# Attention heads in pairs, and gathered expert rows handed out during the one-hot stage

## The chip, the cores and the metric

The kernel runs on one core of a Trainium2 chip. The metric is the device time of one execution in microseconds; lower is better. The engines are named as in the profile: PE multiplies matrices (PEld is its loading of the stationary operand), DVE and ACT are the vector and the scalar engine, POOL is GpSimd, SP issues most transfers. Each engine works through its own instructions in a fixed order and waits on semaphores for the others. Rows of the profile give start and duration in us, or mean durations in ns where a column says so.

## What is computed

Two layers (l = 0, 1) of a hybrid trunk over 512 latent tokens of width 1024 with 256 context tokens. The context goes through layer 0 in full, and gives only keys and values to layer 1. Cut to what matters:

```python
ys, ysc = token_mixers(...)          # four kinds of attention, four heads of width 64 each:
#   y_na: neighbourhood, 512 + 256 keys, a bias per head      y_df: differential, two maps of width 32 a head
#   y_sw: sliding window of 128, with a sink                  y_gq: grouped heads, all 768 keys
x = x + g1 * merge_branches(h, ys, ...)
x = x + g2 * peer_ffn(h2, ...)       # a mixture of 16384 one-row experts
...
def peer_ffn(h, wq, keys, u, v):     # 8 heads, the best 16 experts of each token in each head
    a = gelu(einsum('td,thkd->thk', xb, u[eb]))
    return einsum('thk,thkd->td', gb * a, v[eb])
```

## The kernel before, in words

A tile is 128 tokens: the latents are tiles 0 to 3, the context is tiles 4 and 5. Everything is float32; products that need it are split into a high and a low part (`split`), so that one product is three matmuls: high by high, low by high, high by low.

**Order of the stages.** Context mixers, merge and output projection of layer 0; routing scores of the context; then for layer 0 and for layer 1 the latents' mixers, merge, output projection with norm, routing, a one-hot stage (`dense_weights`), and a dense stage (`dense`). A scheduler orders the instructions of each engine ahead of time by priorities and a simulated time line, not by the order of the program text. So a chain may be written one way and stand another way on the engine.

**Attention (`mixers`).** For each of the four kinds (`typ` 0 to 3, in the order of the reference above) there are two blocks of two heads. The two heads of a block lie in partitions 0 to 63 and 64 to 127 of the queries and keys. Before, the head (`sub`) is the outer loop and the query tile `i` the inner one. One step of a head is: `scores` (six matmuls of 64 contracted rows into the PSUM tile `sps`, three over the 512 latent keys and three over the 256 context keys), `softmax` (a maximum on DVE, an exponential on ACT into `prob`), a scaling of `prob` on ACT, and `pv` (six transposes of `prob` into the PSUM tile `mmps`, copies of these to `pT` by ACT and DVE, and six products of `pT` with the values, which write 64 partitions of the output bank). A float32 product stands as two PE instructions in the trace. There are two `sps` tiles, two `pT` and three `prob`. Kind 1 has two score maps per head, and combines them on DVE.

**Gathered work (`sparse`).** Tiles 4 and 5 (context) and tile 3 do the expert sum by gathering: 256 rows of 512 KB each per tile, 128 of u and 128 of v, fetched by an indirect transfer that POOL issues (line 828), and used by one DVE instruction each (line 839 for u, 841 and 843 for v). A piece is two rows. `tick(n, ins)` hands out n pieces at the place where it stands, and makes their gathers and their DVE instructions wait for the matmul `ins` (`pace`). Ticks stand after each head's `pv` (2.9 pieces, `TICK_A`), in the merge (2.7), and in the dense stage, which divides what is left evenly. The row buffers (`rows`, NROW = 8) hold gathered rows; row j + 8 can be fetched when row j is used. The same buffers hold the activations that layer 1's one-hot stage computes ahead (`acts_ahead`, two per buffer). At the start of layer 0's dense stage the rest of the context's rows and all of tile 3's are left. In layer 1 only tile 3's rows exist, and all of them fall in the dense stage.

**One-hot stage (`dense_weights`).** For tiles 0 to 2 it writes the matrix of expert weights to DRAM: 24 blocks of 16 tokens. Per block POOL makes eight one-hot rows (`oj`, line 895), DVE makes two wide `oj` (line 897) and twelve `oi` (line 907), ACT four `oi`, PE sixteen products (line 909). Beside it run the routing of the next tile on DVE and, in layer 0, the modulation of layer 1 (line 174, whose four quarters write partitions 0, 32, 64 and 96), in layer 1 the activations ahead.

**Dense stage (`dense`).** For each of 128 expert groups: 24 matmuls for the activation (lines 923 to 926, weights `ur`), 18 matmuls into the output (line 985, weights `vr`). `ur` and `vr` (512 KB each) are fetched by SP into three buffers, `wc` (1.5 MB) once in eight groups.

Of the kernel before, what the change touches and what calls it, by code (L numbers as in the profile page):

```python
# [23 lines left out]
GW = 64  # L24
# [9 lines left out]
TICK_M = 2.7  # L34
GS = 2
NROW = 8
# [3 lines left out]
def tile_hybrid_trunk(  # L40
# [235 lines left out]
    def na_bias(l, h, pool):  # L276
        t = pool.tile([P, 16, GW], FT, tag="bias", name="bias", bufs=1)
# [30 lines left out]
    def rope_apply(pool, src, tile_i, nh, dh, o, perm=False):  # L308
# [5 lines left out]
        t = pool.tile([P, 256], FT, tag="ropet", name="ropet")  # L314
# [6 lines left out]
        u = pool.tile([P, 256], FT, tag="ropeu", name="ropeu") if perm else o  # L321
# [28 lines left out]
    def head_scale(pool, src, r, nh, w, o, perm=False):  # L350

        u = pool.tile([P, 256], FT, tag="ropeu", name="ropeu") if perm else o
# [118 lines left out]
    def softmax(pool, S_, W, scale, bias=None, sinkc=None):  # L471

        pt = pool.tile([P, 768], FT, tag="prob", name="prob", bufs=3)
# [26 lines left out]
    def scores(q, r, i, keys, S_):  # L500
# [3 lines left out]
        for kh, kl, k0, n in keys:  # L504
            o = 0
            while o < n:
                step = min(512 - off % 512, n - o)
                k = slice(k0 + o, k0 + o + step)
                mm3(S_[:, off:off + step], q[0][r, t], q[1][r, t], kh[r, k], kl[r, k], True, True)
                off += step  # L510
                o += step
        return off

    def pv(pool, pt, W, vals, o, part, i, lean):

        nb = W // P
        pT = pool.tile([P, 6, P], FT, tag="pT", name="pT", bufs=2)
        b = 0
        while b < nb:
            n = min(4, nb - b)  # L520
            tp = mm_ps()
            for j in range(n):
                PE.transpose(tp[:, j * P:(j + 1) * P], pt[:, (b + j) * P:(b + j + 1) * P], ident)  # L523
            if b and nb > 2 and not lean:
                V.tensor_copy(pT[:, b:b + n, :], tp[:, :n * P].rearrange("p (a c) -> p a c", a=n))
            else:
                S.activation(pT[:, b:b + n, :], tp[:, :n * P].rearrange("p (a c) -> p a c", a=n), AF.Copy)
            b += n
        for j in range(nb):
            last = PE.matmul(o[part:part + 64, i * P:(i + 1) * P], vals[j], pT[:, j, :], start=(j == 0),  # L530
                             stop=(j == nb - 1))
        return last

    def mixers(l, pool, hh, hl, n_tiles, is_ctx, yd, fill):
# [3 lines left out]
        for typ in range(4):  # L538
# [4 lines left out]
            for blk in range(2):  # L543
# [4 lines left out]
                for sub in range(2):  # L548

                    h = blk * 2 + sub if typ < 2 else blk + 2 * sub  # L550
                    part = sub * 64
                    d = slice(part, part + 64)
                    cvals = [cvt[:, j, kb * P + part:kb * P + part + 64] for j in range(2)]
# [658 lines left out]
```

## Time and profile before

| | |
|---|---|
| median of 3 runs | 5221.3 us (5208.61 to 5224.62) |
| the profiled execution | 5226.89 us, its span 5225.1 us |
| busy in the span | PE 86%, DVE 73%, ACT 38%, POOL 34% |
| latents' mixers, layer 0 / layer 1 | 593 us / 440 us |
| one-hot stage, layer 0 / layer 1 | 247 us / 223 us |
| dense stage, layer 0 / layer 1 | 1163 us / 1003 us |

The stages follow each other with little overlap, so that each is read by itself: the busy time of an engine in the stage's window, against the window's length. A PE row's busy time includes the latency of a matmul's end, so the distance from one start to the next tells what a matmul costs in a stream. The granted clock of a window says how far PE ran at its higher level.

### The profile page before, as it was taken

How to read it: one execution, taken by the hardware profiler on the slowest of the kernel's cores; microseconds unless marked ns; L12 is line 12 of the kernel's file. 1: busy time of each engine (PE TensorE's matmuls, PEld its weight loads, DVE VectorE, ACT ScalarE, POOL GpSimd, SP SyncE). 2: the span in 40 equal slices, each digit the busy share in tenths (PEclk: the TensorE clock that was granted, in tenths of full speed). 3: DMA queues.
4: the chain of work that ended last, by engine and by line, in shares of the span. 5: the costliest groups of instructions: out<-in, count | busy, mean ns of one | idle time of the engine just before them, and what ended most of it. 6: DMA issues, size and time to landing. Idle time of an engine off the chain costs nothing.

```text
span 5225.1 us, 70074 instructions
## 1 busy us (share of the span) xinstructions
PE 4511.5 (86%) x24960; PEld 3935.3 (75%) x24960; DVE 3834.7 (73%) x8420; ACT 2008.0 (38%) x3323; POOL 1791.0 (34%) x1414
## 2 busy tenths in 40 slices
PE   6778885599675889999899979899986889999998
PEld 4577765477663678888788878788776779999997
DVE  3457878989979968887778855553479957777777
ACT  3344443242223643333233344452333743333333
POOL 0000045766613755455555400000002724444442
PEclk7788876799887999999999988799998999999999
DMA  5474256889943789998899831003332468888885
GB/s 192 131 189 158 65 204 225 306 291 349 366 149 133 255 296 333 326 353 310 306 316 343 308 115 40 19 25 104 126 115 77 166 208 316 300 301 309 299 306 208
DMA packets 558322, 1167.75 MB, mean 223 GB/s; under 512 B 79316, under 2 KB 329748, under 8 KB 551828
## 3 DMA queue, kind: packets, MB, share of 16 engines
q1 hardware_dynamic: 410516, 626.33, 36.5%
q0 software_dynamic: 147456, 536.94, 28.6%
q8 instruction: 197, 3.23, 0.2%
q14 instruction: 153, 1.25, 0.1%
HBM read 1090.97 MB, written 72.16 MB: 223 GB/s over the span
## 4 chain that ended last, share of the span: by engine, by line
PE 65%; DVE 15%; DMA 11%; issue 4%; ACT 3%; POOL 2%; SPq 0%; DVEq 0%; ACTq 0%; POOLq 0%
PE sps L985 12%; PE mmps L985 6%; PE mmps L152 6%; PE mmps L923 6%; PE mmps L153 6%; PE mmps L924 6%; PE mmps L154 6%; PE mmps L926 6%; DMA vr<-in_uv_dram 4%; PE mmps L530 3%; DVE rows L839 3%; PE sps L152 2%; POOL oj L895 2%; PE mmps L523 2%; DMA raw<-in_ada_w_dram 2%
## 5 line engine op out<-in xcount | busy, mean ns | idle before, releaser
L828 POOL DMA_INDIRECT rows<-in_uv_dram,idx x1024 | 1484.2, 1449 | 2057.9 <-PE mmps L530 694.9
L895 POOL TENSOR_SCALAR oj<-io,dwt 128x128 f32<-128x128 f32 x384 | 306.1, 813 | 1314.0 <-DVE bv L788 1027.5
L843 DVE SCALAR_TENSOR_TENSOR acc<-rows,gt,acc 128x1024 f32<-128x1024 f32 x508 | 650.6, 1281 | 143.3 <-PE mmps L926 140.3
L839 DVE SCALAR_TENSOR_TENSOR rows<-rows,h 128x1024 f32<-128x1024 f32 x512 | 605.0, 1221 | 146.0 <-PE mmps L926 121.9
L141 DVE TENSOR_TENSOR lo<-raw,hi 128x1024 fp32r<-128x1024 f32 x280 | 341.8, 1221 | 347.6 <-ACT hi L140 347.2
L140 ACT ACTIVATE hi<-raw 128x1024 fp32r<-128x1024 f32 x280 | 296.4, 1060 | 587.3 <-PE mmps L153 331.2
L140 ACT ACTIVATE vh<-vr 128x1024 fp32r<-128x1024 f32 x256 | 270.9, 1059 | 524.2 <-DMA vr<-in_uv_dram 235.2
L141 DVE TENSOR_TENSOR vl<-vr,vh 128x1024 fp32r<-128x1024 f32 x256 | 312.5, 1221 | 165.8 <-ACT vh L140 159.3
L140 ACT ACTIVATE uh<-ur 128x1024 fp32r<-128x1024 f32 x256 | 271.0, 1059 | 361.8 <-PE mmps L985 218.5
L923 PE MATMUL mmps<-p0h,uh 128*128 128x384 f32 x1024 | 351.1, 343 | 20.4 <-ACT uh L140 17.2
L141 DVE TENSOR_TENSOR ul<-ur,uh 128x1024 fp32r<-128x1024 f32 x256 | 312.8, 1222 | 60.6 <-ACT uh L140 49.8
L923 PE MATMUL mmps<-p1h,uh 128*128 128x384 f32 x1024 | 350.2, 342 | 3.0 <-ACT gact L927 2.9
L924 PE MATMUL mmps<-p1l,uh 128*128 128x384 f32 x1024 | 351.1, 343 | 0.0
L924 PE MATMUL mmps<-p0l,uh 128*128 128x384 f32 x1024 | 350.7, 342 | 0.0
L985 PE MATMUL sps<-vh,gh 128*128 128x512 f32 x1024 | 288.2, 404 | 68.9 <-ACT vh L140 57.8
L909 PE MATMUL sps<-oi,oj 128*128 128x128 f32 x1536 | 238.4, 302 | 56.7 <-DVE oi L907 26.3
L985 PE MATMUL sps<-vh,gl 128*128 128x512 f32 x1024 | 281.6, 397 | 0.7 <-DVE gl L141 0.7
L909 PEld LDWEIGHTS sps<-oi,oj 128*128 128x128 f32 x1536 | 208.0, 204 | 95.6 <-POOL oj L895 38.3
L985 PE MATMUL sps<-vl,gh 128*128 128x512 f32 x1024 | 274.8, 390 | 1.6 <-DVE vl L141 1.6
L985 PEld LDWEIGHTS sps<-vh,gh 128*128 128x128 f32 x1024 | 192.7, 192 | 101.4 <-ACT vh L140 62.9
L985 PEld LDWEIGHTS sps<-vh,gl 128*128 128x128 f32 x1024 | 196.1, 192 | 47.0 <-DVE gl L141 1.9
L927 ACT ACTIVATE gact<-mmps 128x384 f32<-128x384 f32 x240 | 116.6, 488 | 278.7 <-PE mmps L926 271.9
(346 smaller groups left out, 11459.6 us busy)
## 6 DMA issues: line engine op xcount, KB each, us to landing
ur<-in_uT_dram SPq DMA_DIRECT2D x256, 512.0 KB
vr<-in_uv_dram SPq DMA_DIRECT2D x256, 512.0 KB
raw<-in_ada_w_dram SPq DMA_DIRECT2D x96, 512.0 KB
raw<-in_w_gate_dram SPq DMA_DIRECT2D x96, 512.0 KB
wd<-wt SPq DMA_DIRECT2D x48, 1024.0 KB
wc<-wd SPq DMA_DIRECT2D x32, 1536.0 KB
raw<-in_w_in_dram SPq DMA_DIRECT2D x72, 512.0 KB
raw<-in_wq_dram SPq DMA_DIRECT2D x48, 512.0 KB
```

Source lines behind the costliest of these rows:

```text
L140: S.activation(hi, raw, AF.Copy)
L141: V.tensor_tensor(lo, raw, hi.bitcast(FT), op=OP.subtract)
L152: PE.matmul(o, lh, rh, start=start, stop=False, skip_group_check=True)
L153: PE.matmul(o, lh, rl, start=False, stop=False, skip_group_check=True)
L828: pace(G.indirect_dma_start(out=r, out_offset=None, in_=uvh, in_offset=bass.IndirectOffsetOnAxis(ap=idx[:, s:s + 1], axis=0), element_offs ...
L839: pace(V.scalar_tensor_tensor(r, r, 1.0, h2, op0=OP.mult, op1=OP.mult, accum_out=a[:, j:j + 1]))
L843: pace(V.scalar_tensor_tensor(acc, r, gt[:, j - P:j - P + 1], acc, op0=OP.mult, op1=OP.add))
L895: G.tensor_scalar(oj[:, tj, :], io, t3[:, 1, t + tj:t + tj + 1], None, op0=OP.is_equal)
L909: PE.matmul(pv[:, c8 // 4, :, c8 % 4], oj[:, tj, :], oi, start=True, stop=True)
L923: PE.matmul(pa[:, :TD], uh[:, k, :], hh[:, k, :TD], start=(k == 0), stop=False, skip_group_check=True)
L924: PE.matmul(pa[:, :TD], uh[:, k, :], hl[:, k, :TD], start=False, stop=False, skip_group_check=True)
L985: PE.matmul(acc(t, half), a[:, t * P:(t + 1) * P], b[:, half * 512:(half + 1) * 512], start=(i == 0 and b is vh and a is gh), stop=(i == P ...
```

## The change

It does four things. `scores` takes both heads of a block (for kind 1 both maps of a head) and issues each of their matmuls in turn, one for each head. `pv` takes both heads' `prob`, transposes the one and then the other, and issues their products with the values in turn. The loop over the query tiles is now the outer one, with one tick of 5.8 pieces per pair of heads. The one-hot stage gets a tick of one piece per block of 16 tokens, paced by the block's last product. Buffers: `prob` 3 to 4, `bias` 1 to 2, `y` 2 to 1, `ropet` and `ropeu` 2 to 1, and the row buffers 8 to 7 (so 14 activations ahead in layer 1, not 16).

```diff
+TICK_W = 1.0
 GS = 2
-NROW = 8
+NROW = 7
...
-        t = pool.tile([P, 16, GW], FT, tag="bias", name="bias", bufs=1)
+        t = pool.tile([P, 16, GW], FT, tag="bias", name="bias", bufs=2)
...
-        t = pool.tile([P, 256], FT, tag="ropet", name="ropet")
+        t = pool.tile([P, 256], FT, tag="ropet", name="ropet", bufs=1)
...
-        pt = pool.tile([P, 768], FT, tag="prob", name="prob", bufs=3)
+        pt = pool.tile([P, 768], FT, tag="prob", name="prob", bufs=4)
...
-    def scores(q, r, i, keys, S_):
+    def scores(q, rows, i, keys, Ss):
...
-                mm3(S_[:, off:off + step], q[0][r, t], q[1][r, t], kh[r, k], kl[r, k], True, True)
+                for a, b in ((0, kh), (0, kl), (1, kh)):
+                    for S_, r in zip(Ss, rows):
+                        PE.matmul(S_[:, off:off + step], q[a][r, t], b[r, k], start=(a == 0 and b is kh),
+                                  stop=(a == 1), skip_group_check=True)
...
-    def pv(pool, pt, W, vals, o, part, i, lean):
+    def pv(pool, pts, W, vals, o, i, lean):
...
-            last = PE.matmul(o[part:part + 64, i * P:(i + 1) * P], vals[j], pT[:, j, :], start=(j == 0),
-                             stop=(j == nb - 1))
+            for u in range(2):
+                last = PE.matmul(o[64 * u:64 * u + 64, i * P:(i + 1) * P], vals[u][j], pTs[u][:, j, :],
+                                 start=(j == 0), stop=(j == nb - 1))
...
-                for sub in range(2):
...
-                    for i in range(n_tiles):
...
+                for i in range(n_tiles):
...
+                        Ss = [s_ps() for _ in range(2)]
+                        W = scores(q, [slice(sub * 64, sub * 64 + 64) for sub in range(2)], i, keys, Ss)
+                        for sub, S_ in enumerate(Ss):
...
-                        tick(TICK_A, pv(pool, p0, W, vals, o, part, i, l == 0))
-                    next(ahead, None)
-                    next(fill, None)
-                y = pool.tile([P, T], FT, tag="y", name="y", bufs=2)
+                    tick(2 * TICK_A, pv(pool, probs, W, vals, o, i, l == 0))
+                    if n_tiles == 2 or i % 2:
+                        next(ahead, None)
+                        next(fill, None)
+                y = pool.tile([P, T], FT, tag="y", name="y", bufs=1)
...
-                        PE.matmul(pv[:, c8 // 4, :, c8 % 4], oj[:, tj, :], oi, start=True, stop=True)
+                        last = PE.matmul(pv[:, c8 // 4, :, c8 % 4], oj[:, tj, :], oi, start=True, stop=True)
...
             SY.dma_start(wd[n * (P // WB) + b], wt)
+            tick(TICK_W, last)
```

What the scheduler makes of it is seen in the order of the instructions. On PE, in layer 1's mixers of kind 3 (`kh` and `ck` keys, `q` queries, `pT` transposed weights, `vt` and `cv` values), before:

```order
L153 MATMUL sps_30435<-kl_29692,qh_29361 128x512
L154 MATMUL sps_30435<-kh_29691,ql_29362 128x512
L152 MATMUL sps_30435<-ck3_25769,qh_29361 128x256
L523 MATMUL mmps_30393<-ident_78,prob_30378 128x128 x2
L530 MATMUL mmps_30242<-pT_30354,vt_29623 64x128 x4
L530 MATMUL mmps_30242<-pT_30354,cv3_25771 64x128 x2
```

The six products of one head (`pT_30354`) stand in one row. In the changed program, on the same engine and kind:

```order
L512 MATMUL sps_30174<-ck3_25769,ql_29360 128x256
L512 MATMUL sps_30175<-kh_29691,qh_29359 128x512
L530 MATMUL mmps_30094<-ident_78,prob_30068 128x128 x2
L538 MATMUL mmps_29981<-pT_30076,vt_29623 64x128
L530 MATMUL mmps_30141<-ident_78,prob_30124 128x128 x4
L538 MATMUL mmps_29981<-pT_30087,vt_29623 64x128
L538 MATMUL mmps_29981<-pT_30076,cv3_25771 64x128
L530 MATMUL mmps_30147<-ident_78,prob_30124 128x128 x2
L538 MATMUL mmps_29981<-pT_30087,cv3_25771 64x128
```

The products of the two heads (`pT_30076`, `pT_30087`) now alternate. The scores of this pair do not: all six of `sps_30174` stand ahead of all six of `sps_30175`. Over a latent mixer stage of layer 1, 288 of the 360 products stand directly ahead of one of the other head, where it was 5; of the 504 score matmuls 103 do, where it was 23. (Layer 0: 290 and 93; context: 37 of 64 products and 50 of 120 score matmuls.)

On POOL, in layer 0's one-hot stage, before (`oj` one-hot rows, `rows` gathered rows):

```order
L828 DMA rows_11906<-in_uv_dram,idx_7907 128x1024
L895 TENSOR_SCALAR oj_13949<-io_89,dwt_13930 128x128 x4
L895 TENSOR_SCALAR oj_13984<-io_89,dwt_13930 128x128 x4
L895 TENSOR_SCALAR oj_14039<-io_89,dwt_13930 128x128 x4
L895 TENSOR_SCALAR oj_14074<-io_89,dwt_13930 128x128 x4
```

and in the changed program:

```order
L905 TENSOR_SCALAR oj_14078<-io_89,dwt_13928 128x128 x4
L838 DMA rows_14004<-in_uv_dram,idx_7905 128x1024
L838 DMA rows_14006<-in_uv_dram,idx_7905 128x1024
L905 TENSOR_SCALAR oj_14133<-io_89,dwt_13928 128x128 x4
L905 TENSOR_SCALAR oj_14168<-io_89,dwt_13928 128x128 x4
L838 DMA rows_14100<-in_uv_dram,idx_7905 128x1024
```

Two gathers now stand between the one-hot rows of one block and those of the next, 43 in all; the dense stage of layer 0 issues 357 after them, where it issued 400. On DVE, 46 instructions on gathered rows stand among layer 0's one-hot work in the changed program, 18 in its first 60% and 28 in its last 40%; there was none.

## Rows read from the trace of the kernel before

**Rows 1.** The page: shares of the chain that ended last, by engine.

```profile
PE 65%; DVE 15%; DMA 11%; issue 4%; ACT 3%; POOL 2%; SPq 0%; DVEq 0%; ACTq 0%; POOLq 0%
```

**Rows 2.** Windows: length, then PE, PEld, DVE, ACT, POOL busy (count), clock, DMA share, GB/s.

```profile
54.00:252.00 198.00, 158.07 (x1084) 119.54 (x1084) 83.74 (x292) 79.89 (x222) 0.00 (x0) 0.78 0.44 134
520.00:1113.00 593.00, 435.77 (x2609) 368.66 (x2607) 500.19 (x1247) 229.85 (x486) 270.77 (x204) 0.77 0.61 206
1463.00:1600.00 137.00, 109.86 (x516) 90.06 (x516) 100.58 (x598) 35.87 (x65) 0.59 (x1) 0.91 0.23 72
1600.00:1847.00 247.00, 173.08 (x1260) 131.35 (x1260) 229.55 (x773) 136.23 (x256) 153.51 (x192) 0.86 0.61 217
1847.00:3010.00 1163.00, 1082.42 (x5288) 973.64 (x5288) 914.25 (x1113) 382.82 (x520) 586.84 (x400) 0.97 0.91 322
3086.00:3526.00 440.00, 409.62 (x2607) 350.60 (x2605) 238.52 (x691) 214.34 (x428) 0.00 (x0) 0.86 0.11 32
4209.00:5212.00 1003.00, 989.64 (x4896) 893.08 (x4896) 715.98 (x903) 368.66 (x481) 392.96 (x256) 0.99 0.83 285
```

**Rows 3.** The chain in the mixers, by line: layer 1 (3122 to 3526), layer 0 (557 to 1113).

```profile
by line: PE mmps L530 22.0%; PE mmps L523 12.2%; PE sps L152 8.9%; PE mmps L152 7.0%; PE mmps L154 6.8%; PE mmps L153 6.7%; PE sps L154 6.2%; PE sps L153 6.0%; DVE mx L486 2.3%; DMA bias<-toep 2.1%; issue 1.7%; PE mmps L295 1.5%; ACT prob L
...
by line: DVE rows L839 15.3%; issue 13.0%; PE mmps L530 11.4%; PE mmps L523 7.0%; DMA rows<-in_uv_dram,idx 4.6%; DVE mx L486 4.4%; PE sps L152 4.1%; PE sps L154 2.8%; DVE acc L843 2.7%; PE sps L153 2.7%; PE mmps L152 2.6%; PE mmps L154 2.4%
```

**Rows 4.** Time line of PE: start, us, line, tile, operation, count; layer 1, kind 3.

```profile
3504.24 0.39 PE L153 MATMUL sps<-kl,qh 64*128 64x512 f32 x1
3504.47 0.39 PE L154 MATMUL sps<-kh,ql 64*128 64x512 f32 x1
3504.70 0.27 PE L152 MATMUL sps<-ck,qh 64*128 64x256 f32 x1
3504.81 0.28 PE L153 MATMUL sps<-cl,qh 64*128 64x256 f32 x1
...
3505.14 1.09 PE L530 MATMUL mmps<-pT,vt 128*64 128x128 f32 x8
3506.06 0.60 PE L530 MATMUL mmps<-pT,cv 128*64 128x128 f32 x4
3506.59 0.87 PE L523 MATMUL mmps<-ident,prob 128*128 128x128 f32 x6
```

**Rows 5.** Time line of PE in the context mixers: matmuls of different partitions side by side.

```profile
110.25 0.61 PE L174 MATMUL mmps<-raw,sc 128*2 128x256 f32 x8 [1.71 <-DMA raw<-in_ada_w_dram]
...
138.04 0.40 PE L152 MATMUL sps<-ck,qh 32*128 32x256 f32 x2
138.26 0.29 PE L153 MATMUL sps<-cl,qh 32*128 32x256 f32 x2
```

**Rows 6.** Windows: layer 0 kind 0; layer 1 kind 1; layer 1 kind 3 (columns as rows 2).

```profile
557.00:678.00 121.00, 99.96 (x646) 85.59 (x646) 88.94 (x240) 53.13 (x122) 0.00 (x0) 0.83 0.17 46
3231.00:3374.00 143.00, 132.94 (x688) 110.36 (x689) 80.49 (x212) 63.78 (x120) 0.00 (x0) 0.73 0.06 19
3466.00:3526.00 60.00, 59.40 (x398) 47.06 (x397) 26.99 (x68) 38.99 (x67) 0.00 (x0) 1.00 0.04 10
```

**Rows 7.** Time line of PEld, layer 1 kind 3: idle before a load, in brackets.

```profile
3483.16 0.31 PEld L523 LDWEIGHTS mmps<-ident,prob 128*128 128x128 f32 x3 [0.17 <-issue]
```

**Rows 8.** The page's costliest groups: count, busy us, mean ns of one, idle before.

```profile
L828 POOL DMA_INDIRECT rows<-in_uv_dram,idx x1024 | 1484.2, 1449 | 2057.9 <-PE mmps L530 694.9
...
L843 DVE SCALAR_TENSOR_TENSOR acc<-rows,gt,acc 128x1024 f32<-128x1024 f32 x508 | 650.6, 1281 | 143.3 <-PE mmps L926 140.3
```

**Rows 9.** Windows: the end of layer 0's one-hot stage; 100 us inside layer 1's dense stage.

```profile
1780.00:1847.00 67.00, 57.39 (x392) 52.03 (x390) 56.98 (x146) 54.30 (x102) 50.99 (x74) 1.00 0.59 216
4409.00:4509.00 100.00, 100.00 (x504) 91.14 (x504) 77.70 (x114) 38.56 (x51) 47.70 (x32) 1.00 0.85 297
```

**Rows 10.** Waits in layer 0's dense stage: engine line, waited for, us, times, longest us.

```profile
ACT vh L140 <- DMA vr<-in_uv_dram: 158.6, 52, 14.9
...
PEld sps L985 <- ACT vh L140: 61.7, 15, 8.5
```

More of the change, by code (lines that the diff above doesn't have):

```diff
@@ new lines, in mixers @@
+                heads = [blk * 2 + sub if typ < 2 else blk + 2 * sub for sub in range(2)]
+                biases = [na_bias(l, h, pool) for h in heads] if (typ == 0 and not is_ctx) else None
+                for i in range(n_tiles):
+                    b0, b1 = (max(0, i - 1), min(4, i + 2)) if typ == 2 else (0, 4)
+                    keys, vals = [(*kc, 0, 256)], [[], []]
+                    if not is_ctx:
+                        keys = [(*kv["k"][kb], b0 * P, (b1 - b0) * P)] + keys
+                    for sub in range(2):
+                        d = slice(sub * 64, sub * 64 + 64)
+                        if not is_ctx:
+                            vals[sub] = [kv["v"][kb][:, j, d] for j in range(b0, b1)]
+                        vals[sub] += [cvt[:, j, kb * P + sub * 64:kb * P + sub * 64 + 64] for j in range(2)]
+                    probs = []
+                    if typ == 1:
+                        for sub in range(2):
+                            Ss = [s_ps() for _ in range(2)]
+                            W = scores(q, [slice(sub * 64 + m * 32, sub * 64 + m * 32 + 32) for m in range(2)], i, keys, Ss)
+                            (p0, z0), (p1, z1) = [softmax(pool, S_, W, 32 ** -0.5) for S_ in Ss]
@@ L589, in mixers @@
[L589 to L593 removed]
+                            probs.append(p0)
+                    else:
+                        Ss = [s_ps() for _ in range(2)]
+                        W = scores(q, [slice(sub * 64, sub * 64 + 64) for sub in range(2)], i, keys, Ss)
+                        for sub, S_ in enumerate(Ss):
+                            if typ == 0 and not is_ctx:
+                                b = biases[sub][:, 7 - 2 * i:15 - 2 * i, :].rearrange("p a b -> p (a b)")
+                                p0, z0 = softmax(pool, S_, W, 1.0, bias=b)
+                            elif typ == 2:
+                                if not is_ctx:
+                                    if i > 0:
+                                        V.tensor_tensor(S_[:, :P], S_[:, :P], swm[:, 0, :], op=OP.add)
+                                    if i < 3:
+                                        c = (i - b0 + 1) * P
+                                        V.tensor_tensor(S_[:, c:c + P], S_[:, c:c + P], swm[:, 1, :], op=OP.add)
+                                p0, z0 = softmax(pool, S_, W, 0.125, sinkc=sink_col[l][:, heads[sub]:heads[sub] + 1])
+                            else:
+                                p0, z0 = softmax(pool, S_, W, 1.0)
+                            S.activation(p0[:, :W], p0[:, :W], AF.Copy, scale=z0[:, 0:1])
+                            probs.append(p0)
```

67 lines of the change are left out of this document (18 added, 49 removed).

## The prediction

> **What bounds the kernel now.** I read the page's chain first: two thirds of it is PE, 15% DVE, 11% transfers [rows 1]. That is an average over stages with different limits, so the windows by stage come next, and in each the question is which engine has no time left. In layer 1's mixers it is PE, 410 of 440 us busy against 239 for DVE and 214 for ACT [rows 2], and the chain there is PE nearly throughout: the products with the values (L530) 22.0%, the transposes 12.2%, the score matmuls together 21.1% [rows 3]. In layer 0's mixers the same attention takes 593 us, because DVE carries gathered rows as well: DVE 500 of 593, PE 436 [rows 2], and the chain's first entry is a DVE instruction on a gathered row (15.3%) while L530 is 11.4% [rows 3]. In layer 0's one-hot stage DVE has 230 of 247 us busy and DMA only 0.61 of its time [rows 2]. In the dense stages PE should be the bound: inside layer 1's, 504 matmuls fit in 100 us with PE always busy [rows 9]. By that rate layer 1's 4896 matmuls need 971 us and took 1003, a loss of 32; layer 0's 5288 need 1049 and took 1163, a loss of 114 [rows 2]. The difference of 82 us is transfers: layer 0 gathers 400 rows there and layer 1 256 (the POOL counts), the DMA share is 0.91 against 0.83 [rows 2], and ACT waits 158.6 us for `vr` weights, of which 61.7 us reach PE's loads [rows 10].
>
> So the change touches one place where PE is scarce (layer 1's mixers), one where DVE is (one-hot, layer 0), and one where transfers are (dense, layer 0).
>
> **The products with the values in turn.** Twelve PE instructions of one head take from 3505.14 to 3506.59, 1.45 us, 0.12 each, though each uses half of the output partitions [rows 4]. Can two of them run side by side? The trace has a case: the modulation's matmuls write four different groups of partitions of one bank, and eight of them end within 0.61 us, where four products of the values, one after the other at half that many columns, take 0.60 [rows 4, 5]. So yes, nearly for free. In layer 1, 22.0% of 404 us is 89 us; 288 of 360 now alternate, and alternating halves the time: 89 x 0.8 / 2 = 36 us off PE. Layer 0: 11.4% of 556 us is 63, and by the same 0.8 / 2, 25 us.
>
> **The scores in turn.** The pairing is possible too: score matmuls of two 32-row halves stand as pairs in the context (`x2`, next pair 0.22 us later) [rows 5]. But the scheduler mostly undoes it: only 80 more of the 504 stand next to one of the other head in layer 1, 66 in layer 0. One costs 0.23 us over 512 keys and 0.11 over 256 (distances of starts [rows 4]), 0.17 in the mean; an adjacency saves half of one in a strict alternation and a whole one where it stands alone, so 80 x 0.17 x 0.75 = 10 us in layer 1 and 8 in layer 0.
>
> **How much of that reaches the end.** Layer 1: 46 us of PE at most. Kind 3 has PE 59.4 of 60 us busy and ACT 39 [rows 6], so PE's relief passes through until ACT is next, at 21 us less. Kind 1 is different: PE is at a granted clock of 0.73 there, 133 of 143 us busy [rows 6], that is, partly at its lower level between waits, and a saved matmul is partly a longer wait. I take two thirds, **-31 us** (bounds 0 and -46). Layer 0: only kind 0 is PE's (100 of 121 us, DVE 89 [rows 6]); the rest is DVE's. Half of 33 us, **-17** (bounds +10 and -33: the ticks come at 5.8 pieces instead of 2.9 with 7 row buffers instead of 8, and a burst of twelve rows has DVE wait for the landing of the last five; such landings are 4.6% of the chain now [rows 3]). Context: 64 products at 0.24 us are 15 us, 37 of 64 alternate, which gives 4; 33 more adjacent scores at 0.11 x 0.75 give 3; PE is 158 of 198 busy there [rows 2], so **-5** (0 to -9).
>
> The Trainium skill, TensorEngine Tiling (Array Packing), Key Properties, says that a change of the tiling mode drains the engine and a change of tile does not. The row that bears on it is the 0.17 us of idle PEld where products give way to transposes [rows 7]; the order of layer 1's mixers has 208 such changes where it had 234, so by that rule the sum would be some 26 x 0.17 = 4 us better, and the alternation itself costs nothing.
>
> **Buffers.** `ropet`, `ropeu` and `y` with one buffer each are written and read by DVE in its own order, or wait for a store that has a whole block of time: 0. `bias` of both heads is loaded at once, two waits for two waits: 0. `prob` with four lets both heads be held: 0.
>
> **Gathered rows in the one-hot stage.** 46 DVE instructions of 1.28 us [rows 8] are 59 us in a stage with 17 us of DVE idle, 10 of them in its last 67 us [rows 2, 9]. DVE is full, so they are added nearly whole: **+52 us**. Low end +41, if all idle time is filled. High end +115: if POOL's gathers (1.45 us each [rows 8]) and DVE's instructions do not overlap, 43 x 1.45 are added to 59, since POOL's next one-hot rows stand behind a gather that waits for the block's last product and for a free buffer, and PE waits for these one-hot rows. POOL is busy 51 of the last 67 us already [rows 9].
>
> **What layer 0's dense stage gets back.** 43 gathers fewer, 357 for 400. In proportion, 82 us for 144 rows are 25 us. Two stages cannot tell whether the loss is in proportion; layer 1's at 0.83 of DMA time has none to speak of, and with the waits the clock rises too (0.97 against 0.99 and 1.00 [rows 2, 9]), so I take a little more, **-32**; bounds -15, and -82 where the whole difference goes.
>
> **Seven row buffers.** In layer 1, 14 activations are made ahead and not 16: two of them, 48 matmuls, go into the dense stage at 504 in 100 us, 9.5 us; the one-hot stage of layer 1 gets a part back. **+7**.
>
> **Rows that shift.** By DVE's order 188 rows are done by the end of layer 0's mixers instead of 200, and 29 instead of 11 after the output projection. These 18 rows (23 us) meet 36 us of idle DVE in the routing window [rows 2], and the mixers are lighter by 12: **0** (+8 to -10).
>
> **The sum.** -31 - 17 - 5 + 52 - 32 + 7 = -26 us against the profiled execution's 5226.9 us, which gives 5201; it lies 5.6 us above the median of the runs, so 5195 against 5221.3, 0.5% faster. About 0.3%, 16 us, is what a measurement of this kernel can tell from no change. Hence the forecast: the mixers give some 53 us, and the one-hot tick takes more than the dense stage returns.
>
> **Rivals.**
> *One-hot in series (slower).* Place: POOL's queue in layer 0's one-hot stage. Gathers that wait for the block's last product hold up the next block's one-hot rows, PE waits for these, and DVE waits for PE. Price +115 instead of +52: 5195 + 63 = 5258. For it: POOL's order has two gathers between blocks, and the one-hot rows have three buffers. Against: POOL has 94 us idle in the stage [rows 2]. The change turns slower than before by over 16 us once the stage grows by some 94 us.
> *The mixers gain nothing (slower).* Both `sps` and both `pT` now belong to one pair, so the next pair's scores wait for both exponentials. Kind 1 works so already, with two maps per head, at clock 0.73 [rows 6]. Then 53 us are gone: 5248. Against: the order shows the scores of a pair standing two pairs ahead of its products. The Trainium skill's TensorEngine Tiling page (Performance Considerations, PSUM Bottleneck) says that packing speeds up PE but not the emptying of PSUM, which would lead here; the trace agrees in that ACT is at 39 of 60 us in kind 3 [rows 6], so by that rule no gain there can exceed 21 us.
> *The dense stage falls below the limit of its transfers.* At 2.8 rows per group instead of 3.1 the `vr` waits vanish, as in layer 1 with 2.0: -82 instead of -32, 5145. Against: only 30% of the difference in rows is removed.
> *The whole PE relief arrives* (46, 33 and 7 us): 33 us more, 5162. It would need ACT and DVE to hide in layer 0, too. That the change doesn't do what it says holds for the scores alone and is in the forecast.
>
> **How the numbers follow.** Forecast 45%, with its own range 5170 to 5225; one-hot in series 13%; mixers gain nothing 17%; dense below the limit 15%; the whole relief 10%. The predicted time is the forecast's, 5195. The range reaches into the two slower rivals and to the dense one, 5138 to 5258. Faster by over 0.3% (below 5205.6): 0.6 of the forecast and both fast rivals, 0.52. Slower by over 0.3% (above 5237): a tenth of the forecast and three quarters of the slow rivals, 0.27. Between: 0.21.
>
> **What the changed kernel's profile would show.** Layer 1's mixers near 409 us with the products' instructions in pairs of starts; layer 0's mixers near 576; its one-hot window near 299 with DVE full and about 43 gathers on POOL; its dense window near 1131 with fewer `vr` waits; layer 1's dense window near 1010. I am wrong if the one-hot window grows by under 35 or over 80 us, if the mixers of layer 1 move by less than 10, or if the dense window of layer 0 falls by more than 60.

## The result, and the profile after

The changed kernel takes 5167.2 us (median) against 5222.9 us of the kernel before on the same chip: a ratio of 0.9898, with a 95% interval of 0.9874 to 0.9922. It is some 55 us faster, where 26 were forecast. The profiled execution's span is 5166.2 us, against 5225.1.

The windows of the changed kernel by stage, layer 0's mixers, routing, one-hot stage and dense stage, then layer 1's mixers and dense stage (columns as in [rows 2]: length, PE, PEld, DVE, ACT, POOL busy with counts, granted clock, DMA share, GB/s):

```profile
515.00:1065.00 550.00, 383.33 (x2603) 324.74 (x2602) 483.10 (x1242) 227.54 (x485) 247.70 (x189) 0.75 0.61 208
1412.00:1585.00 173.00, 108.31 (x516) 88.84 (x516) 149.03 (x751) 36.33 (x66) 27.29 (x20) 0.83 0.34 113
1585.00:1877.00 292.00, 220.92 (x1260) 162.58 (x1260) 261.87 (x734) 138.75 (x254) 225.59 (x237) 0.74 0.77 263
1877.00:2974.00 1097.00, 1067.38 (x5298) 968.94 (x5296) 866.31 (x1048) 394.98 (x524) 540.83 (x357) 0.98 0.91 321
3043.00:3463.00 420.00, 373.67 (x2597) 318.25 (x2595) 238.51 (x691) 211.16 (x428) 0.00 (x0) 0.81 0.12 33
4140.00:5166.00 1026.00, 997.95 (x4947) 901.91 (x4946) 727.47 (x953) 377.33 (x490) 397.66 (x257) 0.99 0.82 282
```

To compare, each stage is cut here at its own first matmul, in every kernel. That moves some windows of [rows 2]. Of the kernel before, routing, one-hot and dense stage of layer 0, cut in this way:

```profile
1463.00:1626.00 163.00, 109.86 (x516) 90.06 (x516) 126.20 (x707) 36.18 (x66) 0.59 (x1) 0.85 0.19 60
1626.00:1844.00 218.00, 172.62 (x1258) 131.05 (x1258) 203.92 (x664) 133.59 (x252) 153.51 (x192) 0.90 0.69 245
1844.00:3016.00 1172.00, 1084.98 (x5298) 975.50 (x5298) 920.25 (x1121) 387.23 (x526) 586.84 (x400) 0.97 0.91 321
```

So the span's 59 us come from: layer 0's mixers 594 to 550 (-44), layer 0's dense stage 1172 to 1097 (-75), layer 1's mixers 440 to 420 (-20), the context ahead of them 465 to 460 (-5); and go into the one-hot stage 218 to 292 (+74), the routing 163 to 173 (+10) and layer 1's dense stage 1019 to 1026 (+7). The rest, some -6, is spread over the other stages. The two large numbers of layer 0 nearly cancel.

What became of the products, on PE's time line in layer 1's mixers (start, us, instruction, count; to set beside [rows 4]):

```profile
3444.41 0.98 PE L538 MATMUL mmps<-pT,vt 128*64 128x128 f32 x13
3445.12 0.27 PE L538 MATMUL mmps<-pT,cv 128*64 128x128 f32 x1
3445.22 0.27 PE L538 MATMUL mmps<-pT,vt 128*64 128x128 f32 x1
3445.23 0.27 PE L538 MATMUL mmps<-pT,cv 128*64 128x128 f32 x1
3445.43 0.44 PE L530 MATMUL mmps<-ident,prob 128*128 128x128 f32 x2
```

Sixteen products start between 3444.41 and 3445.43, 1.02 us, where twelve took 1.45: 0.064 each instead of 0.12. So products that accumulate run side by side too, as [rows 5] suggested for others. Over all of layer 1's mixers, the distances of starts between one product and the next sum to 51 us, against 88 before: 37 us less, the 36 of the prediction.

The gathers and the rows' instructions themselves cost what they did [rows 8]:

```profile
L838 POOL DMA_INDIRECT rows<-in_uv_dram,idx x1024 | 1482.6, 1448 | 2058.3 <-ACT prob L576 685.6
L853 DVE SCALAR_TENSOR_TENSOR acc<-rows,gt,acc 128x1024 f32<-128x1024 f32 x508 | 651.3, 1282 | 179.5 <-PE mmps L937 173.3
```

And the waits in layer 0's dense stage, to set beside [rows 10]:

```profile
ACT vh L141 <- DMA vr<-in_uv_dram: 129.9, 42, 12.3
...
PEld sps L996 <- ACT vh L141: 4.4, 3, 2.1
```

The weights are still late for ACT (158.6 before), but hardly any lateness reaches PE's loads: 4.4 us for 61.7.

One caution for all that follows. A stage's length is that of one profiled execution. Kernels with the same instructions in a stage show its scatter: layer 0's mixers in pairs, with 189 gathers, 550 to 559 in six kernels; layer 1's mixers in pairs 403 to 426 in seven. The context's 5 us lie inside it too: 457 to 465 in four kernels with one head after the other, 454 to 461 in six with pairs.

### The profile page after: what moved, and what is told of

Same layout as the page of the kernel before. It is cut to its first block, busy times and chain, and to the rows that moved or that the text cites. A ratio compares the mean times of both kernels' runs of the same rounds, so it can differ in the third digit from the quotient of the medians.

```text
span 5166.2 us, 70076 instructions
## 1 busy us (share of the span) xinstructions
PE 4448.8 (86%) x24960; PEld 3877.2 (75%) x24960; DVE 3835.9 (74%) x8420; ACT 2018.7 (39%) x3323; POOL 1800.4 (35%) x1414
## 5 line engine op out<-in xcount | busy, mean ns | idle before, releaser
L905 POOL TENSOR_SCALAR oj<-io,dwt 128x128 f32<-128x128 f32 x384 | 317.1, 841 | 1250.7 <-ACT dwt L893 1147.2
L919 PE MATMUL sps<-oi,oj 128*128 128x128 f32 x1536 | 284.6, 336 | 76.4 <-POOL oj L905 43.0
L919 PEld LDWEIGHTS sps<-oi,oj 128*128 128x128 f32 x1536 | 242.3, 231 | 132.4 <-issue 57.0
L512 PE MATMUL sps<-kh,qh 64*128 64x512 f32 (+3 forms) x160 | 89.2, 597 | 157.1 <-ACT prob L494 119.5
```

Source lines behind the costliest of these rows:

```text
L512: PE.matmul(S_[:, off:off + step], q[a][r, t], b[r, k], start=(a == 0 and b is kh), stop=(a == 1), skip_group_check=True)
L905: G.tensor_scalar(oj[:, tj, :], io, t3[:, 1, t + tj:t + tj + 1], None, op0=OP.is_equal)
L919: last = PE.matmul(pv[:, c8 // 4, :, c8 % 4], oj[:, tj, :], oi, start=True, stop=True)
```

## The experiments

### The parts alone

**Pairs without the tick**: in the changed kernel, one line of the one-hot stage goes.

```
-            tick(TICK_W, last)
```

> The changed kernel without the piece of gathered work in the one-hot stage; paired heads and seven row buffers stay. Both theories: layer 0's mixers stay near 550 us, layer 1's near 420, the one-hot window of layer 0 (from its first product to its last) falls from 295 back to about 221. They differ in layer 0's dense window. Theory A (rows gathered per group of matmuls decide: 400 rows are late, 355 are not): it goes back to about 1160, and the total is near 5167 - 74 + 71 = 5164, the same as the changed kernel. Theory B (seven row buffers instead of eight hold the gathers back and leave the transfers of the weights more room): it stays near 1095, and the total is near 5167 - 74 + 6 = 5099.

**The tick without pairs**: the kernel before, with its eight row buffers, and the tick behind the block's last one-hot matmul.

```
+TICK_W = 1.0
...
-                        PE.matmul(pv[:, c8 // 4, :, c8 % 4], oj[:, tj, :], oi, start=True, stop=True)
+                        last = PE.matmul(pv[:, c8 // 4, :, c8 % 4], oj[:, tj, :], oi, start=True, stop=True)
...
+            tick(TICK_W, last)
```

> The kernel before with the piece of gathered work per 16 tokens alone; heads one after the other, eight row buffers. One-hot window of layer 0 from 221 to about 295 by both. Theory A (rows per group): dense window of layer 0 from 1163 to about 1090, mixers unchanged, total near 5223 + 74 - 73 = 5224, the same as before. Theory B (seven buffers): dense 1130 at the least, in proportion to the rows, total near 5223 + 74 - 30 = 5267, slower than before by 0.8%.

**Seven row buffers alone:**

```
-NROW = 8
+NROW = 7
```

> The kernel before with seven row buffers instead of eight and nothing else. Theory A (rows per group): layer 0's dense window stays at 1160 to 1170, layer 1's grows by about 6, total 5223 + 7 = 5230. Theory B (seven buffers hold the gathers back): layer 0's dense window falls to about 1095, total near 5160.

Measured against the kernel before: pairs only 0.9951 (0.9933 to 0.9970), tick only 0.9980 (0.9966 to 0.9993), seven buffers alone 1.0066 (1.0046 to 1.0086). One-hot and dense stage of the pairs alone, the same two of the tick alone, and the dense stages of layers 0 and 1 with seven buffers alone:

```profile
1586.00:1809.00 223.00, 174.53 (x1258) 133.33 (x1258) 203.03 (x660) 133.22 (x252) 148.14 (x192) 0.88 0.67 239
1809.00:3007.00 1198.00, 1095.14 (x5299) 983.10 (x5298) 919.88 (x1121) 387.47 (x527) 581.45 (x402) 0.96 0.89 314
```

```profile
1619.00:1914.00 295.00, 219.13 (x1260) 165.68 (x1260) 262.36 (x737) 138.07 (x254) 234.72 (x237) 0.73 0.74 261
1914.00:2998.00 1084.00, 1061.81 (x5298) 963.77 (x5297) 865.58 (x1048) 396.22 (x524) 548.72 (x356) 0.99 0.91 325
```

```profile
1853.00:3040.00 1187.00, 1089.71 (x5300) 978.89 (x5299) 920.17 (x1121) 386.79 (x526) 582.57 (x402) 0.97 0.89 317
4211.00:5237.00 1026.00, 998.17 (x4946) 902.04 (x4945) 727.54 (x953) 377.33 (x489) 397.44 (x256) 0.99 0.82 282
```

The dense stage follows the rows (theory A): with 400 to 402 rows 1172, 1187 and 1198, with 356 and 357 1084 and 1097; between seven buffers and eight it differs by 13 to 26. The pairs alone took 5189 us, 25 more than theory A had, since their dense stage went to 1198 and not to 1160. Seven buffers are no help to the transfers; alone they cost 0.66%, 34 us, where I had 7. Places that grew in the profile: dense stage of layer 0 +15, of layer 1 +7, one-hot stage +7, some 4 in the routing and 3 in the merge. But that profile's whole span is only 13 us longer, because layer 1's mixers took 423 in it (inside the scatter of their order, 423 to 440) and the stage ahead of the routing 7 less; so these places are not shown to be the 34 us. The pairs, with their other buffers, on top of it are worth the step from 1.0066 to 0.9951, 60 us. The tick is worth 28 us with seven buffers and pairs (0.9951 to 0.9898) and 10 with eight buffers and no pairs; why the dense stage gives 101 us in the one case and 88 in the other is within what single profiles scatter.

### What sets the dense stage

**Half the tick**, as below, **and twice the tick**, with 2.0.

```
-TICK_W = 1.0
+TICK_W = 0.5
```

> The changed kernel with half a piece per 16 tokens (24 rows in the one-hot stage of layer 0 instead of 45). Theory A (the dense stage of layer 0 is bound by the bytes moved; a row is 128 x 1024 x 4 bytes = 0.524 MB, and at the 321 GB/s of that stage 1.63 us, as long as PE needs less): dense window 1097 + 21 x 1.63 = about 1131; the one-hot window 292 - 21 x 1.6 = about 258 or, if idle time of DVE takes the first rows free, 245; total between 5155 and 5170. Theory B (a threshold in rows per group between 356 and 400, above which the value weights come late): dense either at 1097 or at 1190, not between; total about 5130 or about 5220.

> The changed kernel with two pieces per 16 tokens (about 92 rows in the one-hot stage instead of 45). Theory A (bytes bound the dense stage): dense window 1097 - 47 x 1.63 = 1020, stopped by what PE needs at about 1040; one-hot window 292 + 47 x 1.5 = 363; total about 5167 + 71 - 57 = 5181. Theory B (below 356 rows the weights are no longer late): dense stays near 1090, one-hot 363, total about 5235.

Half the tick: 5171.0 us, 0.9924 (0.9905 to 0.9943). Twice the tick: 5213.6 us, 1.0000 (0.9987 to 1.0012). One-hot and dense windows of the half, then of the double tick:

```profile
1589.00:1841.00 252.00, 191.10 (x1258) 144.15 (x1258) 232.15 (x710) 134.91 (x252) 190.18 (x214) 0.83 0.73 257
1841.00:2980.00 1139.00, 1077.17 (x5298) 972.66 (x5298) 894.31 (x1076) 387.62 (x526) 555.01 (x379) 0.97 0.91 320
```

```profile
1590.00:1914.00 324.00, 220.90 (x1259) 161.35 (x1260) 295.17 (x768) 138.16 (x254) 269.33 (x262) 0.75 0.79 278
1914.00:3017.00 1103.00, 1065.96 (x5298) 967.78 (x5298) 834.69 (x1020) 398.17 (x524) 501.74 (x332) 0.98 0.88 308
```

The double tick moved 70 rows, not the 92 that I had counted on. Neither theory holds whole. From 402 rows to 379 to 357 the stage goes 1198, 1139, 1097: about 2.2 us per row, on a slope as A said and not in B's one step. From 357 to 332 rows it doesn't fall at all (1103): B's floor, and there DMA drops to 0.88. So there is a slope down to about 355 rows and a floor from there. In the one-hot stage a row costs its DVE time whole: 22 rows +29 us, 45 rows +69, 70 rows +101, or 1.3 to 1.5 us each, with DVE's own 1.28 the larger part. Half the tick and the whole one come to the same time within their intervals; twice the tick pays where nothing is given back any more. The kernel before with fewer rows in the mixers, below, has more rows in this stage, 420, and gives the slope's other end:

```profile
1824.00:3023.00 1199.00, 1088.50 (x5298) 976.28 (x5298) 944.19 (x1161) 388.40 (x526) 608.88 (x420) 0.97 0.91 322
```

That is 27 us for 20 rows more than 1172 with 400, 1.35 each, where theory A of that run has 1205 to 1220.

**Half the bytes**, in the kernel before; each gather fetches 512 of 1024 columns, and the three DVE operations on a row read `twice(r)`, the fetched half two times, so that the other half is left out of the result; those on u now write to `acc` and not to the row:

```
-                pace(G.indirect_dma_start(out=r, out_offset=None, in_=uvh,
+                pace(G.indirect_dma_start(out=r[:, :D // 2], out_offset=None, in_=uvh,
...
+        twice = lambda r: r[:, None, :D // 2].to_broadcast([P, 2, D // 2])
```

> The kernel before, but each gather fetches the first half of a row's columns only, and VectorE reads that half twice, so that its element count stays (the gathered part of the output is thereby another). Theory A (bytes bound layer 0's dense stage): its window falls from 1172 to what PE needs, 1030 to 1050, total near 5090. Theory B (it is the count of gathers and the VectorE work on them that sets it): it stays above 1150, total within 20 us of before.

It takes 5094.3 us, 0.9767 (0.9746 to 0.9787). Its dense stages of layers 0 and 1:

```profile
1814.00:2884.00 1070.00, 1058.77 (x5298) 962.89 (x5297) 924.34 (x1121) 404.53 (x526) 560.21 (x400) 1.00 0.77 253
4075.00:5094.00 1019.00, 991.41 (x4898) 895.40 (x4898) 726.31 (x951) 376.68 (x486) 407.19 (x256) 0.99 0.66 217
```

With all 400 gathers and DVE as busy as before, the stage falls from 1172 to 1070, PE is busy 1059 of these at clock 1.00, and DMA is at 0.77. So the bytes of the gathers hold the stage up, and neither their count nor DVE's work on them. In layer 1, where DMA was at 0.82 before, the same halving gives nothing: 1019 us again. A row is 128 x 1024 x 4 bytes, 0.524 MB; at the stage's 321 GB/s it is 1.63 us of transfers. The slopes measured at a DMA share of 0.89 to 0.91, 1.35 to 2.2 us a row, lie around that price; no run took the slope itself with other bytes. The floor of 1084 to 1103 lies 14 to 33 us above this run's 1070; what holds it there stays open. By the rate of [rows 9], 504 matmuls in 100 us, PE needs 1051 us here, so the floor is 33 to 52 us above PE's need; layer 1's stage, with 256 rows, is 47 above its own. [rows 2] had given 82 us between the two losses; with both stages cut at their first matmul it is 74, and all of it went with 43 of the 144 rows.

### What the pairs gain

**The products head after head** in the changed kernel, and then **scores and products both head after head** (both edits together):

```
-        for j in range(nb):
-            for u in range(2):
+        for u in range(2):
+            for j in range(nb):
```

```
-                for a, b in ((0, kh), (0, kl), (1, kh)):
-                    for S_, r in zip(Ss, rows):
+                for S_, r in zip(Ss, rows):
+                    for a, b in ((0, kh), (0, kl), (1, kh)):
```

> The changed kernel with the value products of the two heads one head after the other instead of in turn; all else stays. Theory A (the products in turn run side by side on PE, and that is what the mixers gained): layer 1's mixers from 420 back to about 440 with PE busy 374 -> 405, layer 0's from 550 to about 570 (the rest of its 43 us are 15 gathered rows that moved to the routing, which stay away), total near 5167 + 40 = 5207. Theory B (the gain is of the order of the work, two heads in flight and ACT and DVE work of one behind PE work of the other, while PE's products cost what they did): mixers stay at 420 and 550 within 5 us, total within 10 us of the changed kernel's.

> The changed kernel with scores and value products of the two heads each one head after the other: what stays of the pairing is its order of the work (both heads' softmax in flight, rows released per pair). Theory A (in layer 1 the order alone gives the gain, running side by side gives nothing): layer 1's mixers 410 to 420 as with the products alone in series (410), layer 0's about 577, total about 5182. Theory B (the scores side by side carry layer 1's gain): layer 1's mixers back to 428 to 440, layer 0's 585, total about 5205.

"In series" stands for pairs whose instructions come one head after the other. Products alone in series: 5181.5 us, 0.9929 (0.9908 to 0.9950). Both in series: 5171.3 us, 0.9921 (0.9896 to 0.9946), which the intervals can't tell from the changed kernel's 0.9898. The mixers of layers 0 and 1 with both in series:

```profile
514.00:1073.00 559.00, 411.73 (x2606) 354.41 (x2605) 478.06 (x1230) 227.54 (x486) 233.81 (x184) 0.78 0.60 200
3047.00:3464.00 417.00, 382.37 (x2604) 331.40 (x2603) 237.14 (x690) 212.41 (x427) 0.00 (x0) 0.89 0.11 33
```

PE does work longer: the distances between products sum to 79 us in layer 1, not 51 (the scheduler still sets 34 products side by side, where the kernel in turn has 287). Yet layer 1's stage is as short, 417, and layer 0's 559 is at the upper end of the scatter in turn. With the products alone in series layer 1's mixers are at 411 and layer 0's at 577, where theory A of that run had 570. In that window 197 gathers fell instead of 184 to 189, and a kernel in turn that also has 197 (eight buffers, below) takes 565; so 12 of the 577 are left that its rows don't explain. In layer 1 the order of the work carries the gain, as theory A of the second run says and theory B of the first, and running side by side, the prediction's own reason, carries nothing that reaches the end. In layer 0 it may carry 5 to 12 us: 559 against a mean of 554 in turn, and 577 against 565.

**Fewer rows in the mixers**, in the kernel before:

```
-TICK_A = 2.9
+TICK_A = 2.7
```

> The kernel before with 2.7 pieces of gathered work per head and tile of the mixers instead of 2.9, nothing else: by its order 185 rows are done at the end of layer 0's mixers instead of 200, as in the changed kernel, and 340 instead of 360 ahead of the dense stage. Theory A (of the 43 us that layer 0's mixers gained, the rows that leave this stage, full of VectorE work, carry 25): its window falls from 593 to about 570, and the dense window grows by 20 rows x 1.63 to 2.4 us, 1172 to 1205 to 1220; total 5216 - 24 + 40 = 5232. Theory B (the order of the pairs carries them): the window stays at 588 or more, total about 5250.

5226.9 us, 1.0016 (0.9998 to 1.0033). Layer 0's mixers:

```profile
515.00:1098.00 583.00, 445.33 (x2610) 377.18 (x2610) 479.88 (x1229) 229.58 (x485) 245.32 (x187) 0.77 0.58 195
```

Between the theories: 17 rows fewer give 11 us, not 25. So at 184 to 189 rows layer 0's mixers take 583 head after head, 559 in pairs with both in series, and 554 in pairs in turn (the mean of six kernels). Of the 44 us, some 11 are rows that left, some 24 the order, some 5 the side-by-side run; 4 more are this profile's 550 against the mean. The products alone in series split it in another way: with 197 gathers 577, against 594 to 596 head after head with 202 to 204, so that the order is worth 10 to 14, by what the rows between cost, and the side-by-side run 12. The order leaves DVE 81 us idle of 559 instead of 103 of 583. Which of its waits that is can't be read cleanly: they are spread over many, and the largest falls are 8 us each, in the waits of gathered rows for PE's products (11.5 to 3.6) and in those for ACT's exponentials behind a softmax's sum (23.6 to 15.4).

### Where PE's relief goes

In layer 1 the waits of PE for the exponentials that release the score buffers, of the kernel before, of the changed kernel, and with both in series:

```profile
PE sps L152 <- ACT prob L483: 8.9, 4, 5.5
PE sps L152 <- ACT prob L493: 7.7, 6, 4.6
```

```profile
PE sps L512 <- ACT prob L494: 17.7, 9, 5.4
PE sps L512 <- ACT prob L484: 10.6, 3, 6.3
```

```profile
PE sps L512 <- ACT prob L494: 15.0, 7, 5.4
PE sps L512 <- ACT prob L484: 8.6, 3, 5.8
```

16.6 us before, 28.3 after, 23.6 in series: of the 12 us that were added, 7 come with the order alone. The Trainium skill, TensorEngine Tiling (Array Packing), Performance Considerations, PSUM Bottleneck, says that "Tiling speeds up TensorE but not PSUM evacuation"; the 5 that the side-by-side run adds agree with it, though another kernel in turn (`TICK_R = 1.5`, below) has 24.5. All 12 are the second rival's mechanism, at part of its price.

The larger part goes with the granted clock. Layer 1's mixers by order, each kernel's window at its clock: head after head 440 and 439 at 0.86, 432 and 428 at 0.88, 423 at 0.90; in pairs with the products in series 411 and 417 at 0.89; in pairs in turn 426 at 0.80, 420 at 0.81, 417 and 412 at 0.83, 409 at 0.84, 404 and 403 at 0.85. Within one order the same instructions take less time at a higher clock, so much so that window times clock is nearly one number for each: 377 to 381 us head after head, 366 and 369 in series, 338 to 347 in turn. Counted at the full clock, then, the order gives some 12 us and the side-by-side run some 26 more; and its clock is lower by just about so much, 0.80 to 0.85 for 0.89. One seventh of the window, in the part where kind 1 stands, of the changed kernel, with both in series, and of another kernel in turn (`TICK_R = 3.0`, below):

```profile
3223.00:3283.00 60.00, 48.53 (x257) 40.48 (x256) 37.34 (x110) 25.80 (x50) 0.00 (x0) 0.65 0.09 27
```

```profile
3226.00:3285.00 59.00, 51.96 (x307) 43.95 (x307) 41.07 (x119) 24.97 (x48) 0.00 (x0) 0.77 0.12 36
```

```profile
3177.00:3234.00 57.00, 49.09 (x319) 42.17 (x318) 40.95 (x119) 24.98 (x48) 0.00 (x0) 0.81 0.13 38
```

In the changed kernel the clock there is 0.65, so that PE spends more of this stretch at its lower level of 1.2 GHz and gets fewer matmuls through (257 for 307 in series); but the other kernel in turn is at 0.81. So kind 1 tells the kernels in turn from each other (403 us against 420), and not the two orders. What does is the seventh before the last, again of the changed kernel, with both in series, and of the kernel before:

```profile
3343.00:3403.00 60.00, 55.84 (x384) 49.26 (x383) 32.78 (x128) 25.45 (x59) 0.00 (x0) 0.80 0.14 40
```

```profile
3345.00:3404.00 59.00, 53.16 (x385) 46.59 (x382) 36.90 (x149) 26.79 (x61) 0.00 (x0) 0.94 0.14 41
```

```profile
3400.00:3463.00 63.00, 59.17 (x448) 52.53 (x447) 40.44 (x164) 33.52 (x76) 0.00 (x0) 0.99 0.14 42
```

There all seven kernels in turn are at 0.79 to 0.86, the two in series at 0.94 and 1.00, and the five with head after head at 0.99 and 1.00. So with shorter products PE waits more and is granted less of its clock, and the relief doesn't reach the end. Drawn on to 0.86, the pairs in turn would take some 400, 40 less than before: an extrapolation from the seven points, not a run. That the clock is the cause, and not a companion of the waits, wasn't tested apart.

### Eight buffers with the pairs, and a better place for the rows

**Eight row buffers**, in the room of the fourth softmax result:

```
-NROW = 7
+NROW = 8
...
-        pt = pool.tile([P, 768], FT, tag="prob", name="prob", bufs=4)
+        pt = pool.tile([P, 768], FT, tag="prob", name="prob", bufs=3)
```

> The changed kernel with eight row buffers again, their room taken from the fourth buffer of the softmax result (three instead of four). If the seventh buffer's loss is real in both orders (seven alone measured 33 us slower than before) and three results are enough for a pair: dense layer 0 about 1085, dense layer 1 about 1019, mixers 550 and 415, total about 5140. If the fourth result is what lets a pair run ahead: mixers of both layers up by 15 to 30 each, and the total 5170 or more.

5172.2 us, 0.9922 (0.9905 to 0.9939): no gain over the changed kernel. The dense stages do give 10 and 8 us back (1087, 1017). Layer 0's mixers take 15 more (565, with 197 rows) and the routing 7 less; layer 1's stay in their scatter, at 417. A fourth result isn't needed there; that in layer 0 the more rows take the gain, and not the missing fourth result, wasn't tested apart.

**Rows in the routing.** By the windows after, DVE is idle 24 of 173 us in layer 0's routing and DMA is at 0.34, with rows in it for the first time. Two kernels move rows there from the one-hot stage, by a tick after each head's top-16 selection in `route_scores`. The first is shown; the second has `TICK_R = 3.0` and no tick in the one-hot stage.

```
-TICK_W = 1.0
+TICK_W = 0.5
+TICK_R = 1.5
...
-                    PE.matmul(p[:, p_ * P:(p_ + 1) * P], q[:, p_, i * P:(i + 1) * P], kt[:, p_, :], start=True, stop=True)
+                    last = PE.matmul(p[:, p_ * P:(p_ + 1) * P], q[:, p_, i * P:(i + 1) * P], kt[:, p_, :], start=True, stop=True)
...
+            tick(TICK_R, last)
```

> The changed kernel with half a piece per 16 tokens in layer 0's one-hot stage and, for the other half, one and a half pieces per head in the routing before it (25 rows are moved from the one-hot stage to the routing, 408 rows done before the dense stage as in the changed kernel). Theory A (a gathered row costs where VectorE is full, and less where it idles: routing 148 of 172 us busy with 19 rows, one-hot 261 of 292): routing 172 + 25 x 1.28 - half of 24 idle us = about 192, one-hot 252, dense 1097, total about 5167 - 20 = 5147. Theory B (rows cost the same everywhere, VectorE's time each): routing 204, one-hot 252, total about 5160.

> The changed kernel with three pieces per head in layer 0's routing and none in the one-hot stage (48 rows moved from there to the routing; 410 done before the dense stage). Theory A: the routing's idle VectorE time takes some of them: 172 + 48 x 1.28 - 12 to 24 = 209 to 221, one-hot 224, dense 1097, total about 5167 - 68 + 43 = 5142. Theory B: routing 234 or more, total about 5160.

Both beat the changed kernel: 5127.0 us, 0.9829 (0.9806 to 0.9853), and 5126.2 us, 0.9830 (0.9808 to 0.9853). Routing, one-hot and dense stage of the second:

```profile
1418.00:1630.00 212.00, 118.68 (x516) 94.41 (x516) 204.15 (x825) 37.92 (x68) 79.10 (x68) 0.79 0.65 214
1630.00:1850.00 220.00, 171.90 (x1258) 129.97 (x1258) 203.90 (x661) 133.45 (x252) 146.75 (x192) 0.89 0.69 242
1850.00:2935.00 1085.00, 1063.52 (x5298) 965.96 (x5298) 863.19 (x1046) 394.96 (x523) 541.21 (x353) 0.99 0.91 323
```

48 more rows cost the routing 39 us (0.8 each), and the 45 that leave the one-hot stage spare it 72 (1.6 each). The first kernel's routing takes 182 and its one-hot stage 253. Theory A holds, by more than it said: in the routing DVE is now busy 204 of 212, so nearly all its idle time took a row, and the one-hot stage loses the clock's fall too (0.89 again for 0.74). Against the changed kernel's profile 12 us more come from the dense stage and 17 from layer 1's mixers, where these two kernels (404 and 403) are the lowest of the seven in turn; why stays open. The best kernel of this study is thus the changed one with its tick in another stage.

## Why the prediction was right, and where not

The direction was right, and the time lies inside the range, just outside the forecast's own, and next to the 5162 of the rival in which the whole PE relief arrives; but it was not that rival's mechanism that brought it there. That the total lies inside the range is partly luck, since its terms missed in both directions. One of the prediction's own signs of being wrong was met: layer 0's dense window fell by 75, more than 60. By the terms of the sum:

- **Layer 1's mixers**, -31, measured -20 on the two profiles and on the means of five and seven kernels (432 to 413). The step on PE was right for the products (36 forecast, 37 measured off their distances). The step "two thirds of it reach the end" was not a fair sizing of anything: with the side-by-side run taken out, 411 and 417 stay, as much as in turn. The 20 are the order of two heads' work, which I had costed at nothing, and PE's relief goes with waits and a lower clock. I had read the clock in kind 1 (0.73) and noted that a saved matmul is partly a longer wait, and then priced it at a third.
- **Layer 0's mixers**, -17, measured -44. The failed step is "half of 33 us": it took PE's relief as the only source. Rows that left gave some 11, the order 10 to 24, the side-by-side run 5 to 12.
- **One-hot stage**, +52, measured +74. Its base was a little wrong: the window 1600 to 1847 held 26 us of the routing, and with them idle DVE time that the stage itself doesn't have (14 us of 218, not 17 of 247). The 46 rows' 59 us are added whole, and 10 to 15 more in waits and at a clock of 0.74 for 0.90. The series rival (+115) didn't come: POOL is busy 226 of 292, beside DVE. A little of its mechanism did: PE's waits for POOL's one-hot rows rose from 12.1 to 25.8 us. Its price was added up wrongly, too: 43 x 1.45 and 59 are 121; 115 is 63 on top of the forecast's 52.
- **Layer 0's dense stage**, -32, measured -75, near the bound of -82. The third rival came in its own stage, at nearly its price. The failed step is the price of a row. I divided the stage's loss against layer 1 by the difference in rows, 0.57 us each, and called that proportional. But the rows that matter are the last ones, above the point where transfers are covered: each of these costs about its bytes, 1.63 us at 321 GB/s, and the trace of before had what was needed for that price, DMA at 0.91 in the mean of the stage [rows 2]. 43 x 1.63 is 70. The rival's reason, the weights no longer late for PE, is the same event seen from PE: 61.7 to 4.4 us.
- **Seven buffers**, +7, measured 34 alone. I followed the activations made ahead in layer 1 (+7, right to the microsecond: 1019 to 1026) and left out what a smaller stock of rows may do where rows are gathered; layer 0's dense stage grew by 15 with seven buffers alone. Which stages hold the whole 34 stays open.
- **Shifted rows**, 0, measured +10 in the routing; some 20 rows there cost less than half of their DVE time (10 of 25 us), so they had met idle time, but not for nothing.
- **Context**, -5, measured -5, which is inside the scatter of that stage and confirms nothing.

So a forecast of -26 met -59 on the profiles by errors of both signs: 43 us in the dense stage and 27 in layer 0's mixers too cautious, 22 in the one-hot stage, 11 in layer 1's mixers and 10 in the routing too hopeful, and 6 in stages that I had left at nothing. What the missing eighth buffer costs is inside these stages' numbers.

## What to carry to other kernels

Where a stage shows its DMA near full throughout (0.91 here), price a transfer that leaves it at its bytes over the stage's own GB/s, and look for the floor: here the rows from 357 down to 332 gave nothing. Before moving work, list each stage's idle time on the engine that the work needs, with stages cut at their own first instruction: here a row cost 1.6 us in one stage and 0.8 in the stage ahead of it. And when a change reorders work and also makes it cheaper, run the reordering alone; here it alone gave all that the pairs gained in layer 1's mixers, and a good part of what they gained in layer 0's.

## What was not expected of the hardware

Two accumulating fp32 products into different halves of the output partitions, fed in turn, start 0.064 us apart in a run of sixteen instead of 0.12, and over the whole stage their distances sum to 51 us instead of 88. Where they ran so, PE's granted clock in layer 1's mixers was 0.80 to 0.85 and not 0.86 to 0.90, and within one order of instructions the stage's time went with the clock: 426 us at 0.80, 403 at 0.85. And halving the bytes of each gather, with as many gathers and as much DVE work, shortened the kernel by 2.3%: of layer 0's dense stage, 102 of 1172 us were the gathers' bytes. Layer 1's, at a lower DMA share, stayed at 1019.
